# Where the values of two attention mixers get their norm scale: on GpSimd before the transposes, or on ScalarE behind them

## The chip, the cores and the metric

The kernel runs on one core of a Trainium2 chip. A core has five engines that work side by side, each with its own queue of instructions that it takes in order: TensorE (PE, matmuls and transposes; its weight loads are listed as PEld), VectorE (DVE), ScalarE (ACT), GpSimd (POOL) and SyncE (SP). An instruction that waits holds up everything behind it on its engine. Data comes from memory by DMA transfers, which are issued from SP, ACT and POOL. Matmul results land in PSUM and have to be taken out of it before its space can be used again.

The metric is the device time of one execution in microseconds (us). Lower is better. The kernel of before has a median of 891.46 us over three runs.

## The reference, cut to what matters

One step of a one-layer decoder for 512 prompt tokens and 8 sample tokens, the latter with caches. Two attention mixers read the same normalised input; their outputs are gated, summed and projected, and a channel mixer follows.

```python
def _rmsnorm(x, g):
    return x * rsqrt(mean(x * x, axis=-1) + NORM_EPS) * g     # one root per token

h = _rmsnorm(x, norm1_g)
z = h @ w_in                           # (tokens, 1024) x (1024, N_IN)
qa, ka = rope(z[q, k of mixer A])      # 16 query heads, 2 key heads of 64
va     = z[v of mixer A]               # 2 heads: 128 columns
qb, kb = rope(z[q, k of mixer B])      # 3 groups of 4 heads: 768 columns each
vb     = z[v of mixer B]               # 768 columns, no rope
# mixer A: 128 keys back, with sinks.  mixer B: group g looks back 128 keys in
# steps of 1, 4 or 16; the three outputs are weighted by their softmax sums.
# returned as well: the new cache rows, that is the k and v of the last tokens
```

The root is one number per token, and a product with a weight is linear. So the root may be left out of h and multiplied into z's rows later, in any place before the values are used.

## The kernel before, in words

**Layout.** Activations stand transposed: features on the 128 partitions, tokens along the free axis, 520 columns (512 of the prompt, 8 of the sample). `h_hi` and `h_lo` are the two parts of the input times `norm1_g`, without the root. The roots exist twice: `st[:, 10:15]`, token-major (a token per partition, one column for each of four blocks of 128 and one for the sample), and `spread`, 128 x 520, where each column holds its token's root in all 128 partitions. `cos` and `sin` have been multiplied by `spread`, so queries and keys get the root with their rotation. Values have no rotation.

**Projections.** w_in is worked through in chunks of 128 columns: qb0 to qb5, kb0 to kb5, vb0 to vb5, ka, va, qa0 to qa7, and then the gates (ga, gb) and output projections. A weight chunk is loaded (`raw_...`), split by ACT and DVE into `whi_...` and `wlo_...`, and multiplied with three matmuls for each of 8 slices of the input and each of two spans of 256 and 264 columns: 48 matmuls into a PSUM tile `ps` with the chunk's name (psvb4 is that of vb4; L292, L293, L295). The pool of these tiles, mm, has two buffers. Score tiles (sb, sa, and the small qs, ks, vs) share two buffers, transposes to token-major (tt, tsb, tps, tb) share a single one, `ps_t`.

**Values.** `evac_v` takes a value chunk out of PSUM with ACT into the work tile z and multiplies it by `spread` on POOL (L489). For the chunks of groups 1 and 2 (vb2 to vb5, `blocked`) ACT copies to a spare tile `zr` first (L492), and POOL writes z in a column order by residue of four, once for the sample's 8 columns (L493) and once for the 512 others (L494). The work tiles z and zs have two buffers each and are shared with the rotations of the keys and queries and with some gates. Then `b_tokens` and `a_tokens` transpose z four times on PE (L510, tile `tt_vb...`), ACT copies the 128 x 512 result to its place with tokens on the partitions (L561), and the 8 sample columns are transposed (L563, `vs...`) and copied by DVE. These steps are not run at once but put in the list `later`, which is worked off near the end of the next projection, so that PE has matmuls ahead of them.

**The cached scores.** Between the chunks kb0 and vb1 runs a loop over six pieces of mixer B's cache, `bs_step`: a load of queries from DRAM spread over 128 partitions (`qc`, issued by POOL, one buffer, L581), POOL's product `kc` (L586) and DVE's reduction (L587). The next qc load can start when the product is done. Behind the last piece, `bs_softmax` transposes the scores in three groups `tsb` (L607), each copied by DVE (L608) from the one `ps_t` buffer, and ACT takes the exponentials. `bs_probs` transposes the result (`tps`, L622), and DVE copies it (L623).

**Later places.** Mixer B's prompt attention follows (scores `sb` at L812 and L816), laid between the projections of va and qa. Then its tiles are closed, and mixer A starts with its scores `sa` (L946, reduced by DVE at L950), while the sample's cached keys `kca` are loaded (L1003, issued by SP), rearranged by POOL (`kpm`, L1009) and completed by a DVE copy into `kta` (L1017).

**What sets the order.** The program text gives the dependencies and a first order; a scheduler that simulates the engines fixes the order of each engine's queue when the kernel is built. So an edit at one place can change the order of instructions elsewhere, and the chip follows that order.

Of the kernel before, what the change touches and what calls it, by code (L numbers as in the profile page):

```python
# [9 lines left out]
F32 = mybir.dt.float32  # L10
F32R = mybir.dt.float32r
BF16 = mybir.dt.bfloat16
AF = mybir.ActivationFunctionType
ALU = mybir.AluOpType
AX = mybir.AxisListType

P = 128
D = 1024
NK = 8
NS = 8  # L20
NP = 512
T = NS + NP
# [44 lines left out]
def trunk_kernel(tc, x_prompt, x_sample, cache_a, cache_b1, cache_b2, cache_b3, norm1_g, w_in, sinks,  # L67
                 w_pa, w_pb, w_o, norm2_g, w_gu, w_down, final_g, cos_d, sin_d, mask_a_d, mask_b_d, mask_r_d,
                 y_p, y_s, o_pa, o_pb1, o_pb2, o_pb3, o_sa, o_sb1, o_sb2, o_sb3):
    nc = tc.nc  # L70
# [6 lines left out]
    base = root.enter_context(tc.tile_pool(name="base", bufs=1, side="left"))  # L77
# [14 lines left out]
    ident = base.tile([P, P], F32, name="ident")  # L92
# [5 lines left out]
    epst = base.tile([P, 1], F32, name="epst")  # L98
    nc.vector.memset(epst, EPS)
    g2 = base.tile([P, NK], F32, name="g2")  # L100


    copies = []
# [174 lines left out]
    later = []  # L278
# [147 lines left out]
    def norm_spread():  # L426
        for js in ((0, 1, 2, 3), (4,)):
            c0, c1 = blocks[js[0]][0], blocks[js[-1]][0] + blocks[js[-1]][1]
            bc = bank_of(f"spr{js[0]}")
            for i, j in enumerate(js):  # L430
                c, n, _ = blocks[j]
                nc.tensor.matmul(bc[:, c - c0:c - c0 + n], ones[:n, :], xstat[j][:n, :n], start=(i == 0), stop=True, skip_group_check=True)
            nc.vector.tensor_copy(spread[:, c0:c1], bc[:, :c1 - c0])
        nc.gpsimd.tensor_tensor(cos, cos, spread, op=ALU.mult)
        nc.vector.tensor_tensor(sin, sin, spread, op=ALU.mult)
# [13 lines left out]
    with tc.issue_after(steps[1, AFT[2], "a"]), tc.issue_after(steps[1, AFT[3], "v"]):  # L449
        for j in range(5):  # L450
            norm_square(j)
        norm_roots()
        norm_spread()
    nc.sync.dma_start(x_spill, x_t)
    n1ctx.close()

# [28 lines left out]
    def evac_v(ps2, name, blocked):  # L485
        z = work.tile([P, T], F32, tag="z", name="z_" + name)
        if not blocked:
            nc.scalar.activation(z, ps2, AF.Copy)
            nc.gpsimd.tensor_tensor(z, z, spread, op=ALU.mult)  # L489
        else:  # L490
            zr = work.tile([P, T], F32, tag="zs", name="zr_" + name)
            nc.scalar.activation(zr, ps2, AF.Copy)  # L492
            nc.gpsimd.tensor_tensor(z[:, NP:], zr[:, NP:], spread[:, NP:], op=ALU.mult)  # L493
            nc.gpsimd.tensor_tensor(z[:, :NP].rearrange("p (c q) -> p q c", c=4), zr[:, :NP].rearrange("p (q c) -> p q c", c=4),  # L494
                                    spread[:, :NP].rearrange("p (q c) -> p q c", c=4), op=ALU.mult)
        return z

    def unperm(ap):

# [42 lines left out]
    def b_tokens(ch, z):  # L542
        g, pr = divmod(ch, 2)
        sl = slice(pr * P, pr * P + P)

        def keys():
            ts_ = ps_s.tile([P, 512], F32, tag="s", name=f"ks{ch}")
            nc.tensor.transpose(ts_[:NS, :P], kb[:, ch, NP:], ident)
            nc.vector.tensor_copy(nat(kvb_s[:, g, 0, sl]), unperm(ts_[:NS, :P]))
            if g == 0:  # L550
                tv = to_tokens(kb[:, ch], [384], f"kb{ch}")
                nc.vector.tensor_copy(nat(k1_l[:, sl]), unperm(tv[:, 0]))
            else:
                tv = to_tokens(kb[:, ch], QORD, f"kb{ch}")
                for c in range(4):
                    nc.scalar.activation(nat(kv23[:, g - 1, c, 0, sl]), unperm(tv[:, c]), AF.Copy)

        def values():
            tv = to_tokens(z, QORD, f"vb{ch}")
            dst = v1[:, :, sl] if g == 0 else kv23[:, g - 1, :, 1, sl]  # L560
            nc.scalar.activation(dst, tv, AF.Copy)  # L561
            ts_ = ps_s.tile([P, 512], F32, tag="s", name=f"vs{ch}")
            nc.tensor.transpose(ts_[:NS, :P], z[:, NP:], ident)  # L563
            nc.vector.tensor_copy(kvb_s[:, g, 1, sl], ts_[:NS, :P])

        return keys if z is None else values

# [118 lines left out]
    def q_tokens():  # L686
# [6 lines left out]
                nc.vector.tensor_copy(nat(qb_s[:, g, pr * P:pr * P + P]), unperm(ts_[:NS, P * i:P * i + P]))  # L693
        nc.gpsimd.dma_start(q_dram, qb_s)

    later.append(q_tokens)
    loaded = {}

    def bs_step(n):
# [34 lines left out]
    def a_tokens(z):  # L734
        def go():
            tv = to_tokens(z, QORD, "va")
            nc.scalar.activation(va, tv, AF.Copy)
            tv = to_tokens(ka, [384], "ka")
            nc.vector.tensor_copy(nat(ka_l), unperm(tv[:, 0]))
            ts_ = ps_s.tile([P, 512], F32, tag="s", name="vsa")  # L740
            nc.tensor.transpose(ts_[:NS, :P], z[:, NP:], ident)
            nc.tensor.transpose(ts_[:NS, P:2 * P], ka[:, NP:], ident)
            nc.vector.tensor_copy(kva_s[:, 1], ts_[:NS, :P])
            nc.vector.tensor_copy(nat(kva_s[:, 0]), unperm(ts_[:NS, P:2 * P]))
            nc.gpsimd.dma_start(o_pa[0, 0, :, 0].rearrange("t h d -> t (h d)"), ka_l)
            nc.gpsimd.dma_start(o_pa[0, 0, :, 1].rearrange("t h d -> t (h d)"), va[:, 3])
            nc.gpsimd.dma_start(o_sa[0, :, 127].rearrange("b a h d -> b a (h d)"), kva_s)
        return go
# [863 lines left out]
```

## Time and profile before

| what | value |
|---|---|
| runs of before | 889.6, 891.46, 892.64 us; median 891.46 |
| profiled execution | 895.41 us |
| its span (first to last instruction) | 893.6 us |
| mean granted clock of TensorE | 0.985 |
| PE busy | 860.5 us (96%) |
| PE weight loads busy | 810.0 us (91%) |
| DVE busy | 536.5 us (60%) |
| ACT busy | 380.0 us (43%) |
| POOL busy | 175.9 us (20%) |

The profile is of one execution, the one of 895.41 us. A row of a group or of a timeline gives the start in us from the beginning of the span, the length in us (busy time of the group where there are several), the engine, the line of the kernel and the operation as result <- operands; `x4` means four alike in a row. In square brackets stands how long the engine was idle before, and what ended this. A row of a window begins with its start and end and the sum of the busy time; behind it come the busy times of PE, PEld, DVE, ACT and POOL, each with its number of instructions, then the granted clock as a share of full speed, the DMA engines' share and GB/s.

### The profile page before, as it was taken

How to read it: one execution, taken by the hardware profiler on the slowest of the kernel's cores; microseconds unless marked ns; L12 is line 12 of the kernel's file. 1: busy time of each engine (PE TensorE's matmuls, PEld its weight loads, DVE VectorE, ACT ScalarE, POOL GpSimd, SP SyncE). 2: the span in 40 equal slices, each digit the busy share in tenths (PEclk: the TensorE clock that was granted, in tenths of full speed). 3: DMA queues.
4: the chain of work that ended last, by engine and by line, in shares of the span. 5: the costliest groups of instructions: out<-in, count | busy, mean ns of one | idle time of the engine just before them, and what ended most of it. 6: DMA issues, size and time to landing. Idle time of an engine off the chain costs nothing.

```text
span 893.6 us, 16990 instructions
## 1 busy us (share of the span) xinstructions
PE 860.5 (96%) x6868; PEld 810.0 (91%) x6868; DVE 536.5 (60%) x1053; ACT 380.0 (43%) x782; POOL 175.9 (20%) x142
## 2 busy tenths in 40 slices
PE   6998989999999999999999799999999999999995
PEld 6898889787989888877999799999999999999995
DVE  4878638656478556552554559777534777773433
ACT  6423314434458455442332336454313455543322
POOL 2335553444325122240000021110000000000001
PEclk9999999999999999999999899999999999999998
DMA  9646755665678761599999617999985988999652
GB/s 298 183 126 183 216 167 161 196 171 143 150 177 223 206 172 30 142 240 220 288 249 283 178 48 198 322 318 284 334 306 174 329 274 273 313 320 323 217 188 96
DMA packets 166790, 194.75 MB, mean 218 GB/s; under 512 B 6936, under 2 KB 141224, under 8 KB 165304
## 3 DMA queue, kind: packets, MB, share of 16 engines
q1 hardware_dynamic: 141256, 99.40, 38.5%
q10 hardware_dynamic: 13216, 67.06, 20.6%
q0 software_dynamic: 12240, 27.22, 15.5%
q8 instruction: 54, 0.88, 0.4%
q14 instruction: 24, 0.20, 0.1%
HBM read 186.81 MB, written 93.81 MB: 314 GB/s over the span
## 4 chain that ended last, share of the span: by engine, by line
PE 79%; DMA 8%; DVE 6%; POOL 2%; issue 2%; ACT 1%; POOLq 0%; SPq 0%; ACTq 0%; DVEq 0%
PE pse L1511 3%; PE poa L978 3%; PE pse L1512 3%; PE pse L1514 3%; PE psb L1365 2%; PE psa L1367 2%; PE pse L1365 2%; PE psb L1367 2%; PE pse L1367 2%; PE psb L1366 2%; PE psa L1365 2%; PE pse L1366 2%; PE psa L1366 2%; DMA raw_wo<-in_w_o 2%; DMA qc<-q_dram 2%; PE psqa L292 2%
## 5 line engine op out<-in xcount | busy, mean ns | idle before, releaser
L1332 ACT ACTIVATE whi<-rawp 128x1024 fp32r<-128x1024 f32 x94 | 97.7, 1041 | 144.2 <-PE psb L1366 35.4
L1333 DVE TENSOR_TENSOR wlo<-rawp,whi 128x1024 fp32r<-128x1024 f32 x94 | 112.8, 1201 | 44.0 <-ACT whi L1332 40.1
L1511 PE MATMUL pse<-g,whi 128*128 128x260 f32 x192 | 52.6, 291 | 0.7 <-DVE x L1499 0.7
L1512 PE MATMUL pse<-g,whi 128*128 128x260 f32 x192 | 50.7, 282 | 0.0
L960 POOL TENSOR_TENSOR pa<-pa,sta 128x1024 f32<-128x1024 f32 (+1 forms) x16 | 29.6, 1848 | 93.6 <-DVE sta L959 60.7
L1366 PE MATMUL psb<-ht_lo,whi 128*128 128x260 f32 x160 | 45.2, 283 | 0.0
L1367 PE MATMUL psb<-ht_hi,wlo 128*128 128x260 f32 x160 | 45.2, 283 | 0.0
L1365 PE MATMUL psb<-ht_hi,whi 128*128 128x260 f32 x160 | 45.2, 283 | 0.0
L1365 PE MATMUL psa<-hb_hi,whi 128*128 128x260 f32 x160 | 45.1, 282 | 0.0
L1367 PE MATMUL psa<-hb_hi,wlo 128*128 128x260 f32 x160 | 45.1, 283 | 0.0
L1366 PE MATMUL psa<-hb_lo,whi 128*128 128x260 f32 x160 | 45.0, 281 | 0.0
L292 PE MATMUL pso<-m_hi,whi_wo 128*128 128x260 f32 x128 | 36.3, 294 | 4.6 <-DVE x L1142 4.6
L1514 PE MATMUL pse<-g,wlo 128*128 128x260 f32 x192 | 40.7, 283 | 0.0
L1511 PEld LDWEIGHTS pse<-g,whi 128*128 128x128 f32 x192 | 36.2, 188 | 1.0 <-DVE x L1499 0.9
L292 PE MATMUL psqa<-h_hi,whi_qa 128*128 128x256 f32 (+1 forms) x128 | 36.6, 304 | 0.0
L1425 POOL DMA_DIRECT2D yts<-in_final_norm_g x1 | 0.6, 590 | 181.5 <-PE psb L1367 181.5
L1512 PEld LDWEIGHTS pse<-g,whi 128*128 128x128 f32 x192 | 36.2, 188 | 0.0
L293 PE MATMUL pso<-m_lo,whi_wo 128*128 128x260 f32 x128 | 36.2, 292 | 0.0
L293 PE MATMUL psqa<-h_lo,whi_qa 128*128 128x256 f32 (+1 forms) x128 | 35.8, 298 | 0.0
L292 PE MATMUL psga<-h_hi,whi_ga 128*128 128x256 f32 (+1 forms) x128 | 34.9, 293 | 0.3 <-ACT whi_ga L182 0.3
L293 PE MATMUL psga<-h_lo,whi_ga 128*128 128x256 f32 (+1 forms) x128 | 34.7, 289 | 0.0
L293 PE MATMUL psgb<-h_lo,whi_gb 128*128 128x256 f32 (+1 forms) x128 | 34.5, 287 | 0.0
(446 smaller groups left out, 3102.8 us busy)
## 6 DMA issues: line engine op xcount, KB each, us to landing
rawp<-in_w_gu SPq DMA_DIRECT2D x30, 512.0 KB, 7.0
rawp<-in_w_down SPq DMA_DIRECT2D x16, 512.0 KB, 6.7
out<-in_cache_b_kv ACTq DMA_DIRECT2D x8, 1022.0 KB, 7.7
out<-in_cache_b_kv ACTq DMA_DIRECT2D x8, 512.0 KB, 5.1
raw_qa<-in_w_in SPq DMA_DIRECT2D x8, 512.0 KB, 7.8
raw_ga<-in_w_in SPq DMA_DIRECT2D x8, 512.0 KB, 8.0
raw_gb<-in_w_in SPq DMA_DIRECT2D x8, 512.0 KB, 6.2
raw_pa<-in_w_pa SPq DMA_DIRECT2D x16, 256.0 KB, 11.6
```

Source lines behind the costliest of these rows:

```text
L292: nc.tensor.matmul(ps[i], hi[:, k], xh[:, k0 + k, sl], start=st, stop=False)
L293: nc.tensor.matmul(ps[i], hi[:, k], xl[:, k0 + k, sl], start=False, stop=False)
L960: last_pool[0] = nc.gpsimd.tensor_tensor(p[:, :, m0:], p[:, :, m0:], st[:, 5].unsqueeze(2).to_broadcast([P, 4, 256 - m0]), op=ALU.mult).ins
L978: nc.tensor.matmul(po[64 * kv:64 * kv + 64, :], va[:, j - 1 + r, 64 * kv:64 * kv + 64], pts_[kv, r], start=(r == rel[0]), stop=(r == 1), s ...
L1332: a = nc.scalar.activation(hi, raw, AF.Copy)
L1333: nc.vector.tensor_tensor(lo, raw, hi.bitcast(F32), op=ALU.subtract)
L1365: nc.tensor.matmul(pss[e], h, xh[:, j, i], start=start and i == 0, stop=False, skip_group_check=True)
L1366: nc.tensor.matmul(pss[e], h, xl[:, j, i], start=False, stop=False, skip_group_check=True)
L1367: nc.tensor.matmul(pss[e], l, xh[:, j, i], start=False, stop=i == 3, skip_group_check=True)
L1511: nc.tensor.matmul(ps[h], hi[:, k], gh[:, sl], start=st, stop=False)
L1512: nc.tensor.matmul(ps[h], hi[:, k], gl[:, sl], start=False, stop=False)
L1514: nc.tensor.matmul(ps[h], lo[:, k], gh[:, slice(*SPAN2[h])], start=False, stop=en)
```

## The change

The values are transposed as they come out of the matmuls. The root is applied behind the transpose, when ACT copies them: there a token stands on each partition, and an ACT copy takes a scale per partition.

- A tile `roots` (128 x 9) is added: columns 0 to 3 hold the roots of the prompt's tokens in plain order, column 8 those of the sample, both copied by DVE from `st`. Columns 4 to 7 hold the roots in the order by residue. They come from `strided_roots`: four PE transposes of `spread` and one DVE copy, put in `later` behind `q_tokens`.
- `evac_v` loses POOL's products: 11 instructions. For the blocked chunks, ACT writes z itself, in two pieces and with the strided order, without `zr`.
- The copy behind the transposes (`scaled`) is four ACT instructions of 128 x 128, each with a column of `roots` as its scale, instead of one of 128 x 512; seven times.
- The copies of the sample's values become DVE multiplications by `roots[:NS, 8:9]`.

```diff
+    roots = base.tile([P, 9], F32, name="roots")
...
         norm_spread()
+        nc.vector.tensor_copy(roots[:, 0:4], st[:, 10:14])
+        nc.vector.tensor_copy(roots[:NS, 8:9], st[:NS, 14:15])
...
         z = work.tile([P, T], F32, tag="z", name="z_" + name)
         if not blocked:
             nc.scalar.activation(z, ps2, AF.Copy)
-            nc.gpsimd.tensor_tensor(z, z, spread, op=ALU.mult)
         else:
-            zr = work.tile([P, T], F32, tag="zs", name="zr_" + name)
-            nc.scalar.activation(zr, ps2, AF.Copy)
-            nc.gpsimd.tensor_tensor(z[:, NP:], zr[:, NP:], spread[:, NP:], op=ALU.mult)
-            nc.gpsimd.tensor_tensor(z[:, :NP].rearrange("p (c q) -> p q c", c=4), zr[:, :NP].rearrange("p (q c) -> p q c", c=4),
-                                    spread[:, :NP].rearrange("p (q c) -> p q c", c=4), op=ALU.mult)
+            nc.scalar.activation(z[:, NP:], ps2[:, NP:], AF.Copy)
+            nc.scalar.activation(z[:, :NP].rearrange("p (c q) -> p q c", c=4), ps2[:, :NP].rearrange("p (q c) -> p q c", c=4), AF.Copy)
         return z
+
+    def scaled(dst, tv, first):
+        for c in range(4):
+            nc.scalar.activation(dst[:, c], tv[:, c], AF.Copy, scale=roots[:, first + c:first + c + 1])
...
             tv = to_tokens(z, QORD, f"vb{ch}")
             dst = v1[:, :, sl] if g == 0 else kv23[:, g - 1, :, 1, sl]
-            nc.scalar.activation(dst, tv, AF.Copy)
+            scaled(dst, tv, 4 if g else 0)
             ts_ = ps_s.tile([P, 512], F32, tag="s", name=f"vs{ch}")
             nc.tensor.transpose(ts_[:NS, :P], z[:, NP:], ident)
-            nc.vector.tensor_copy(kvb_s[:, g, 1, sl], ts_[:NS, :P])
+            nc.vector.tensor_scalar_mul(kvb_s[:, g, 1, sl], ts_[:NS, :P], roots[:NS, 8:9])
...
+    def strided_roots():
+        tp = ps_t.tile([P, 512], F32, tag="t", name="trt")
+        for c in range(4):
+            nc.tensor.transpose(tp[:, P * c:P * c + P], spread[:, c:NP:4], ident)
+        nc.vector.tensor_copy(roots[:, 4:8], tp.rearrange("p (c f) -> p c f", f=P)[:, :, 0])
+
     later.append(q_tokens)
+    later.append(strided_roots)
...
             tv = to_tokens(z, QORD, "va")
-            nc.scalar.activation(va, tv, AF.Copy)
+            scaled(va, tv, 0)
...
-            nc.vector.tensor_copy(kva_s[:, 1], ts_[:NS, :P])
+            nc.vector.tensor_scalar_mul(kva_s[:, 1], ts_[:NS, :P], roots[:NS, 8:9])
```

Behind the new tile the lines move by one to eleven: L489 becomes L491, L510 becomes L514, L608 becomes L612, L622 becomes L626, L812 becomes L823, L950 becomes L961 and L1017 becomes L1028.

The edit also moves other instructions. Three places show it; a number behind a name is only that of the buffer, and the brackets name the engines or DMA queues that a row waits for.

**POOL, in the loop of the cached scores while the chunks vb0 and vb1 run.** Before:

```order
L581 DMA qc20_1118<-q_dram_314 128x4x256 [waits Pool_49]
L489 TENSOR_TENSOR z_vb0_1270<-z_vb0_1270,spread_111 128x520 [waits Activation_49]
L586 TENSOR_TENSOR kc20_1116<-kc20_1116,qc20_1118 128x1024 [waits DMAHW6_49,DMASW6_49]
L581 DMA qc24_1199<-q_dram_314 128x4x256 [waits Pool_49]
L489 TENSOR_TENSOR z_vb1_1340<-z_vb1_1340,spread_111 128x520 [waits Activation_49]
L586 TENSOR_TENSOR kc24_1197<-kc24_1197,qc24_1199 128x1024 [waits DMAHW0_49,DMASW7_49]
L796 DMA out_7<-kvb_s_311 8x512 [waits DVE_49]
```

After:

```order
L585 DMA qc20_1127<-q_dram_317 128x4x256 [waits Pool_49]
L590 TENSOR_TENSOR kc20_1125<-kc20_1125,qc20_1127 128x1024 [waits DMAHW6_49,DMASW6_49]
L585 DMA qc24_1208<-q_dram_317 128x4x256 [waits Pool_49]
L590 TENSOR_TENSOR kc24_1206<-kc24_1206,qc24_1208 128x1024 [waits DMAHW0_49,DMASW7_49]
L807 DMA out_7<-kvb_s_314 8x512 [waits DVE_49]
```

The two products with `spread` no longer stand between the load of a piece and the work on the pieces.

**PE, where chunk ka ends and va begins.** Before, the transposes of vb3 and vb4 and those of vb5's sample columns stand spread within va's 48 matmuls; this is the piece around the first of them:

```order
L295 MATMUL psva_1780<-h_hi_104,wlo_va_1687 128x264
L292 MATMUL psva_1780<-h_hi_104,whi_va_1686 128x256
L293 MATMUL psva_1780<-h_lo_105,whi_va_1686 128x256
L292 MATMUL psva_1780<-h_hi_104,whi_va_1686 128x264
L293 MATMUL psva_1780<-h_lo_105,whi_va_1686 128x264
L510 MATMUL tt_vb3_1585<-ident_84,z_vb3_1525 128x128 [waits DVE_49]
L510 MATMUL tt_vb3_1585<-ident_84,z_vb3_1525 128x128 x3
L295 MATMUL psva_1780<-h_hi_104,wlo_va_1687 128x256
L295 MATMUL psva_1780<-h_hi_104,wlo_va_1687 128x264
```

After, they stand together ahead of va's first matmul, with the twelve small transposes `tps` and a first group of mixer B's scores:

```order
L626 MATMUL tps_1525<-ident_84,sr_319 128x8 x8
L296 MATMUL pska_1704<-h_hi_105,wlo_ka_1623 128x256
L296 MATMUL pska_1704<-h_hi_105,wlo_ka_1623 128x264
L514 MATMUL tt_vb3_1597<-ident_84,z_vb3_1539 128x128 [waits DVE_49]
L514 MATMUL tt_vb3_1597<-ident_84,z_vb3_1539 128x128 x3
L514 MATMUL tt_vb4_1677<-ident_84,z_vb4_1615 128x128 [waits Activation_49]
L514 MATMUL tt_vb4_1677<-ident_84,z_vb4_1615 128x128 x3
L567 MATMUL vs5_1750<-ident_84,z_vb5_1697 8x128 [waits Activation_49]
L823 MATMUL sb000_1869<-kb_310,qb_309 32x256 x4
L827 MATMUL sb000_1869<-kb_310,qb_309 128x128 x2
L293 MATMUL psva_1797<-h_hi_105,whi_va_1700 128x256 [waits Activation_49]
```

Two matmuls of ka are left between `tps` and the transposes of vb3, and none between those of vb3 and of vb4.

**DVE, where mixer A's first scores are reduced.** Before:

```order
L474 STREAM_SHUFFLE zs_qa7_2805<-z_qa7_2804 128x520 [waits Activation_49]
L950 ISA pa000_2859,sta000_2860<-sa0000_2861,mask_a_112 128x128 [waits PE_49]
...
L950 ISA pa000_2859,sta000_2860<-sa0001_2874,mask_a_112 128x128
L950 ISA sta000_2860 128x1
L1017 COPY kta_3128<-ka_293 128x8 [waits DMAHW6_49,Pool_49]
L938 TENSOR_TENSOR qs011_3044<-qa_292,qs011_3044 64x512 [waits Activation_49]
```

After:

```order
L477 STREAM_SHUFFLE zs_qa7_2824<-z_qa7_2823 128x520 [waits Activation_49]
L1028 COPY kta_3147<-ka_296 128x8 [waits DMAHW6_49,Pool_49]
L961 ISA pa000_2878,sta000_2879<-sa0000_2880,mask_a_113 128x128 [waits PE_49]
...
L961 ISA pa000_2878,sta000_2879<-sa0001_2893,mask_a_113 128x128
L961 ISA sta000_2879 128x1
L949 TENSOR_TENSOR qs011_3063<-qa_295,qs011_3063 64x512 [waits Activation_49]
```

The copy into `kta`, which waits for the load of `kca` and for POOL, has moved ahead of the four reductions.

## The prediction

> **What bounds the kernel now.** I read the page's totals first, then the list of what PE waited for, then the chain that ended last in 80 to 270 us.
>
> ```profile
> span 893.6 us, 16990 instructions
> PE 860.5 (96%) x6868; PEld 810.0 (91%) x6868; DVE 536.5 (60%) x1053; ACT 380.0 (43%) x782; POOL 175.9 (20%) x142
> ...
> PE pso L292 <- DVE x L1142: 4.6, 1, 4.6
> PE tt_vb L510 <- POOL z_vb L489: 3.3, 2, 2.5
> ```
>
> PE is busy for 860.5 of 893.6 us. An edit here pays only where PE stands still, or where its clock is low. POOL, which loses work, is busy 20% of the time: the scaling taken off it is worth nothing by itself. What counts is the 3.3 us for which PE waited for that scaling.
>
> ```profile
> 103.92 3.31 POOL kc L586
> 107.51 6.28 DMA qc<-q_dram
> 113.87 2.41 POOL kc L586
> 117.37 1.30 POOL z_vb L489
> 118.72 0.66 PE tt_vb L510 x4
> 124.83 0.44 PE tsb L607 x4
> 128.48 0.44 PE tsb L607 x4
> 129.64 0.24 PE psvb L295 x2
> 130.37 0.24 PE psvb L295 x2
> 144.62 0.84 PE tps L622 x12
> 153.82 0.57 PE sb L812 x8
> 154.39 0.64 PE sb L816 x4
> 181.22 1.68 PE pos L660 x16
> 248.10 11.32 DMA kca<-in_cache_a_kv
> 259.59 1.25 POOL kpm L1009 x2
> ```
>
> This is the chain in order of time (start, length). Up to 118.7 it isn't PE's: it is the loop of the cached scores, a qc load of some 6 us, POOL's product kc, the next load. The scaling of chunk vb1 is queued behind it, and PE behind the scaling. From 118.7 to 248 the chain is PE alone, six projection matmuls in 0.73 us (129.64 to 130.37), 0.12 each. At 248.10 it leaves PE for the load of kca.
>
> **The stall that goes.**
>
> ```profile
> 109.68 0.66 PE L510 MATMUL tt_vb<-ident,z_vb 128*128 128x128 f32 x4 [0.79 <-POOL z_vb L489]
> 118.72 0.66 PE L510 MATMUL tt_vb<-ident,z_vb 128*128 128x128 f32 x4 [2.53 <-POOL z_vb L489]
> 109.66 0.58 ACT L488 ACTIVATE z_vb<-psvb 128x520 f32<-128x520 f32 x1
> 120.00:124.00 4.00, 4.00 (x23) 4.00 (x22) 1.23 (x2) 0.01 (x1) 2.69 (x2) 0.57 0.86 277
> ```
>
> ACT had vb1's copy ready at 110.24, so without POOL's product neither group of transposes waits: 0.79 + 2.53 = 3.32 us. The last row is a window: PE busy all 4.00 us, yet at a granted clock of 0.57. It stands right behind the 2.53 us gap, so I let it go with the gap: 4.00 x 0.43 = 1.72 us. Together PE gains 5.04 us by the middle of chunk vb4.
>
> [...]
>
> **What is late next.** PE now runs into the same qc loop at another place. The three groups of tsb share one PSUM tile, so the second waits for DVE's copy of the first (L608), and that copy stands in DVE's queue behind the last cached reduction (L587).
>
> ```profile
> 121.31 2.36 POOL L586 TENSOR_TENSOR kc<-kc,qc 128x1024 f32<-128x1024 f32 x1 [2.65 <-DMA qc<-q_dram]
> 123.70 1.22 DVE L587 TENSOR_REDUCE st_b<-kc 128x16 f32<-128x1024 f32 x1 [2.77 <-POOL kc L586]
> 125.31 0.68 DVE L608 COPY sr<-tsb 8x512 f32<-8x512 f32 x1 [0.39 <-PE tsb L607]
> ```
>
> POOL's last product started when its load landed, not when POOL was free, so it stays where it is, L587 ends at 124.92 and the copy at 125.60. PE comes to its first transposes at 118.72 - 3.32 = 115.40, adds 0.52 for them and 37 rows of 0.12 (tsb stands 5 rows later now), 0.44 for tsb, 27 rows: 124.04. It waits 1.56 us. So of 5.04 us, 3.48 are left. A lower price (0) needs an earlier load; a higher one has no row.
>
> The four new transposes of the spread tile and DVE's copy of them cost PE about 0.44 us (as tsb's four), some 60 us earlier, and POOL no step. They only use up part of that 1.56 us wait: nothing. If they delayed the loop itself, they would cost up to 0.44 + 0.68.
>
> **The values' chain, vb3 to vb5.** Two things change on ACT.
>
> ```profile
> 104.73 0.79 ACT L556 ACTIVATE kv<-tt_kb 128x128 f32<-128x128 f32 x4 [1.34 <-PE tt_kb L510]
> 148.78 0.60 ACT L561 ACTIVATE kv<-tt_vb 128x512 f32<-128x512 f32 x1 [0.60 <-PE tt_vb L510]
> 191.83 0.18 ACT L664 ACTIVATE ob_hi<-pos 128x16 fp32r<-128x16 f32 x1
> L492 ACT ACTIVATE zr_vb<-psvb 128x520 f32<-128x520 f32 x4 | 2.3, 584 | 0.0
> L861 ACT ACTIVATE ob_hi<-pob 128x512 fp32r<-128x512 f32 x2 | 2.2, 1113 | 5.7 <-PE pob L855 5.7
> 145.50 0.26 DVE L623 COPY pts<-tps 128x96 f32<-128x96 f32 x1 [1.42 <-PE tps L622]
> ```
>
> The token copy is four activations of 128x128 instead of one of 128x512: 0.79 for 0.60, seven times, +1.3 us of ACT. The blocked evacuation (four chunks) is two activations: 0.18 for the 8 samples, and 128x512 with a strided result, between 0.584 (L492, plain) and 1.113 (L861, strided, the nearer): +0.2 to +0.7 each. In all +2 to +4 us on an engine that is busy 43%. The cover is that ACT waits for PE around here; where it is gone is one place.
>
> Before, ACT emptied psvb5 into a spare tile at once. Now it writes z itself, which has two buffers, so the evacuation of vb5 waits until PE has transposed vb3; it stands in ACT's queue ahead of the copy for vb4 and of z_ka, and va's projection takes over vb5's PSUM tile. The new order therefore puts tps, tt_vb3, tt_vb4, vs5 and a score group ahead of psva, with hardly a projection row between. On PE: tps ends; DVE's copy takes 0.04 + 0.26, and about 0.1 to be seen, two rows (0.24) lie beside it: 0.2 idle. After tt_vb3 (0.44), tt_vb4 waits for four scaled copies, 0.79 + 0.2 of passing on, about 1.1 idle. The evacuation, 0.18 + 1.11, runs beside tt_vb4 (0.44) and the score group (0.57 + 0.64): nothing more is lost if vs5, between them, needs only the 8 samples' part, up to 0.75 if it needs all. Lower end 0.9 (the short waits hidden), upper 2.1; I take 1.5, as the strided row is the nearer one.
>
> **The kca barrier.** DVE's kta copy (L1017) waits for kca's load and POOL's kpm; it moves ahead of the first four score reductions (L950).
>
> ```profile
> 257.03 0.28 DVE L950 CUSTOM_DVE_ANT_0 pa<-sa,mask_a 128x128 f32<-128x128 f32 x1
> 260.86 1.26 DVE L1017 COPY kta<-ka 128x8 f32<-128x8 f32 x1 [2.30 <-POOL kpm L1009]
> 258.81 0.23 PE L946 MATMUL sa<-k_hi,qs 128*128 128x128 f32 x1
> 265.94 0.39 PE L946 MATMUL sa<-k_hi,qs 128*128 128x256 f32 x1 [1.75 <-DVE sta L950]
> 266.00:270.00 4.00, 4.00 (x22) 4.00 (x23) 3.80 (x19) 3.84 (x14) 1.29 (x2) 0.61 0.69 165
> ```
>
> Counted from 248.10, where kca starts, DVE did L950 from +8.9 to +10.5, waited, and had kta done at +14.0. In the new order it idles from +8.9, has kta at +14.0 and only then the reductions. The score tiles have two buffers, so PE's third group (now at +10.7, as 258.81) waits for the first reduction: to +14.5, 3.7 us. The group that waited 1.75 us at +17.8 then comes at +18.4 (14.0, the reductions with zs between 1.5, 2.4 of other rows, 0.4) with 11 projection rows (1.3) fewer done. Loss 0.6 + 1.3 = 1.9 us. If kca lands early, the loss is a gain of the old 1.75 and of the slow stretch behind it (4.00 x 0.39 = 1.6); if the longer gap costs a second slow stretch, the loss is 1.9 + 1.6 = 3.5. I take 1.9.
>
> **Sum.** -5.04 + 1.56 + 0 + 1.5 + 1.9 = -0.1 us. The profiled execution took 895.41 us for its span of 893.6; it would take 895.3. The median of the three runs, 891.46, lies 3.95 us under that execution; I carry the difference over: **891.4 us**, no change. About 0.3%, 2.7 us, is what a measurement of this kernel can tell.
>
> **Rivals.** *Faster, the barrier opens early.*
>
> ```profile
> raw_qa<-in_w_in SPq DMA_DIRECT2D x8, 512.0 KB, 7.8
> raw_ga<-in_w_in SPq DMA_DIRECT2D x3, 512.0 KB, 9.7
> ```
>
> kca is 512 KB and took 11.32 us; others of that size took 7.8 (page) and 9.7 (three issues just ahead of kca). At 9.7 the barrier's loss is 0.3, 889.8. It decides below about 8.7 us; at 7.8 DVE finds kpm ready and the result is 891.46 - 3.48 + 1.5 - 3.35 = 886.1. I price it at 887.5. For it: the new order puts fewer rows between psqa6 and this point, so other transfers move. Against: those transfers move with kca.
>
> *Slower, the clock.* One mechanism: short or narrow matmuls lower the granted clock even where PE never waits.
>
> ```profile
> 184.00:189.00 5.00, 5.00 (x30) 4.97 (x30) 3.80 (x7) 1.72 (x3) 1.62 (x2) 0.66 1.07 223
> ```
>
> This window follows the 16 tiny matmuls of 181.22. The new cluster tps to sb, 4.8 us with two gaps, is of the same kind, and the kca gap is longer: two stretches of 1.7 us more, 894.8. It decides when both fall. Against: later score groups lie further apart in the new order, and the old stretch at 185 may go.
>
> *The change doesn't do what it says:* tt_vb still waits, now for ACT, where z_vb stands behind a weight split of about 1 us. Then the 5.04 is lost, but also the 1.56: 895 us. Against it, ACT's row at 109.66 is 5 us early.
>
> *Given back later:* PE stands 4.6 us before pso at 506, behind weight loads. If these keep their hour, an earlier PE gains nothing there, but none is forecast.
>
> **How the numbers follow.** Forecast (-2.7 to +2.7) 0.42. Early barrier 0.25, and 0.04 for both terms of loss hidden without it (888.0): faster 0.29. Clock 0.23, doesn't do it 0.06: slower 0.29. The likeliest case's own range is 888.8 to 894.1. To leave out no more than 2 in 10, the range reaches into the early barrier to 887.2 and into the clock to 895.2.
>
> **What would show it.** Right: no wait of tt_vb on POOL; a wait of the second tsb on L608's copy of 1 to 2 us, with PE 3 to 4 us earlier there; idle PE of 1 to 2 us between tps and psva; DVE waiting over 3 us at kta, and PE at the third score group. Wrong: kca landing in under 9 us, psva directly behind pska without a gap, or more than one slow stretch more or fewer up to 280 us.

## The result, and the profile after

The changed kernel takes 898.54 us in the median of four runs (892.49 to 904.32), the kernel before 890.53 us beside it. The ratio is 1.0101, with a 95% interval of 1.0056 to 1.0146: **slower**, where no change (891.4) was forecast and 895.2 was the upper end of the range. A repeat (below) has a median of 899.12 us over twelve runs, against 890.34 for the kernel before, a ratio of the medians of 1.0099; five of its executions lie over 900 us and are left out of the ratio and interval that are given there, since the comparison drops what is over 1.5% above the fastest.

The profiled execution is one of the shorter ones: 894.56 us, span 892.8, clock 0.985, against 895.41, 893.6 and 0.985 of the one before. So the two totals say nothing here, and the profile has to be read by place. First the waits of PE in the changed kernel (who waited for what: us in all, times, longest):

```profile
PE ta L981 <- ACT pta L983: 9.2, 1, 9.2
PE xtp L403 <- DMA xt<-in_x_prompt: 6.2, 2, 3.5
...
PE pso L293 <- ACT whi_wo L183: 1.6, 1, 1.6
...
PE tt_vb L514 <- ACT z_vb L493: 1.2, 1, 1.2
```

The wait of tt_vb on POOL is gone, and so is that of sa on DVE (1.75 before). A wait of 9.2 us stands on top, at a place of which the forecast said nothing: mixer A's last transposes, near 391 us. (`ta` is the PSUM tile of these transposes and `pta` ACT's copy of it; `poa` is mixer A's output, `pa` and `ga` name weights and tiles of the projections around it, and `pso` is the tile of the last projection of this part, near 460 to 530 us.) The timelines of POOL, SP, ACT and PE there show its parts:

```profile
376.98 1.89 POOL L971 TENSOR_TENSOR pa<-pa,sta 128x1024 f32<-128x1024 f32 x1 [7.59 <-DVE sta L970]
378.81 3.76 POOL L142 DMA_DIRECT2D sum_s1B<-in_w_gu  x3
379.89 0.37 SPq L165 DMA_DIRECT2D raw_ga<-in_w_in  x1
398.70 1.06 ACT L183 ACTIVATE whi_ga<-raw_ga 128x1024 fp32r<-128x1024 f32 x1 [11.41 <-DMA raw_ga<-in_w_in]
399.66 0.58 ACT L983 ACTIVATE pta<-ta 128x512 f32<-128x512 f32 x1
400.39 1.09 PE L981 MATMUL ta<-ident,pa 128*128 128x128 f32 x4 [9.19 <-ACT pta L983]
```

POOL finishes mixer A's last product and issues three transfers that add weight columns into `sum_s1B` in memory, 768 KB each. One us later SP issues the load of the second late gate's weights, `raw_ga`, 512 KB. It lands after 18.7 us. ACT's split of it (L183) stands in ACT's queue ahead of the copy of the transposed probabilities (`pta`), and PE stands behind that copy. The same four places before:

```profile
384.13 0.37 SPq L164 DMA_DIRECT2D raw_ga<-in_w_in  x1
388.01 2.87 POOL L960 TENSOR_TENSOR pa<-pa,sta 128x1024 f32<-128x1024 f32 x1 [4.19 <-ACT whi_ga L182]
388.45 1.06 ACT L182 ACTIVATE whi_ga<-raw_ga 128x1024 fp32r<-128x1024 f32 x1 [0.58 <-DMA raw_ga<-in_w_in]
390.82 3.74 POOL L141 DMA_DIRECT2D sum_s1B<-in_w_gu  x3
```

There the load was issued at 384.13 and had landed (4.2 us) before the adds began at 390.82. The change brought the load 4.2 us forward and the adds 12.0 us. Most of these 12 us are order: before, two weight splits of ACT (whi_pb6 and whi_pb7) stood between mixer A's last two groups of exponentials; now four splits stand behind the last group. ACT's row right behind the last exponentials, before and in the changed kernel:

```profile
386.25 0.57 ACT L972 ACTIVATE pta<-ta 128x512 f32<-128x512 f32 x1
```

```profile
374.27 0.58 ACT L983 ACTIVATE pta<-ta 128x512 f32<-128x512 f32 x1
```

POOL's product follows the exponentials, and the adds, which wait for nothing else, follow the product.

The theory taken into the runs, **collision**: the change itself is worth about nothing, as the sum had it, and the loss comes from these adds, which now run into a weight load. Rivals: **luck** (one slow load in one execution), and **bytes** (the stage from 380 to 512 us is bound by its loads, so that PE's lead is given back there in any case).

### The profile page after: what moved, and what is told of

Its sections match the earlier page's. It is cut to its first block, busy times and chain, and to the rows that moved or that the text cites. A ratio compares the mean times of both kernels' runs of the same rounds, so it can differ in the third digit from the quotient of the medians.

```text
span 892.8 us, 17018 instructions
## 1 busy us (share of the span) xinstructions
PE 857.5 (96%) x6872; PEld 807.2 (90%) x6872; DVE 532.7 (60%) x1056; ACT 385.3 (43%) x807; POOL 164.9 (18%) x131
## 4 chain that ended last, share of the span: by engine, by line
PE 83%; DMA 5%; DVE 5%; issue 2%; POOL 1%; ACT 1%; POOLq 0%; SPq 0%; ACTq 0%; DVEq 0%
PE pse L1522 3%; PE pse L1523 3%; PE poa L989 3%; PE pse L1525 3%; PE psb L1376 2%; PE psa L1378 2%; PE psb L1377 2%; PE psb L1378 2%; PE pse L1377 2%; PE psa L1377 2%; PE psa L1376 2%; PE pse L1378 2%; PE pse L1376 2%; DMA raw_ga<-in_w_in 2%; PE psgb L296 2%
## 5 line engine op out<-in xcount | busy, mean ns | idle before, releaser
L1523 PE MATMUL pse<-g,whi 128*128 128x260 f32 x192 | 50.9, 282 | 0.0
L968 ACT ACTIVATE pa<-pa,sta 128x256 f32<-128x256 f32 (+1 forms) x64 | 30.0, 471 | 15.3 <-DVE sta L964 15.2
L293 PE MATMUL psgb<-h_hi,whi_gb 128*128 128x256 f32 (+1 forms) x128 | 34.4, 288 | 0.0
```

What stands on the lines that cost most here:

```text
L293: nc.tensor.matmul(ps[i], hi[:, k], xh[:, k0 + k, sl], start=st, stop=False)
L968: nc.scalar.activation(p[:, i, m0:], p[:, i, m0:], AF.Exp, bias=st[:, 1, i:i + 1], scale=SC, accum_out=st[:, 4, i:i + 1])
L1523: nc.tensor.matmul(ps[h], hi[:, k], gl[:, sl], start=False, stop=False)
```

## The experiments

A result lists for each execution its span and its mean granted clock. Span times clock is taken as an estimate of what the span would have been at full clock, and the rest of the span as one of what the slow clock cost; below, "full" and "slow" are these two, as means over a run's executions (a span of 887.0 at 0.987 is 875.5 and 11.5).

### The collision: the same again, held, and put into the kernel before

**e1, the changed kernel once more**, no edit.

> The changed kernel once more, for a second profile and more times. Collision theory: the change brings PE some 7 us ahead by 386 us and mixer A's last POOL product 11 us ahead (377 instead of 388 us); the three 768 KB adds into sum_s1B that stand behind it in POOL's queue now start one us ahead of the load of raw_ga, which takes 18.7 us instead of 4.2, and PE waits 9.2 us plus about 2 at the halved clock. It is in the order of the program, so it must show again: an idle PE of 5 to 11 us around 391 us behind a load of raw_ga of over 12 us; times 892 to 904, median 1.0 to 1.5% over the kernel before. Luck theory (one slow load in one execution): no such wait, raw_ga lands in under 9 us, times within 0.3% of before.

Measured: 899.12 us over twelve runs (886.71 to 905.57), ratio 1.0041 (1.0001 to 1.0081). The profiled execution was the shortest of the twelve, and has the wait too:

```profile
PE ta L981 <- ACT pta L983: 8.9, 1, 8.9
```

Not luck. Over all twelve, full is 881.9 and slow 14.1, against 879.0 and 10.0 of the 29 runs of the kernel before beside it: 2.9 us are lost at full clock and 4.1 by the clock. Over the seven executions up to 900 us it is 881.3 and 11.1, a loss of 2.3 and 1.1. So this run puts the loss somewhere between 3 and 9 us, and not all of the 9 us wait reaches the end: at pso, where PE waited 4.6 us before, it waits 2.2 in the first profile of the changed kernel and not at all in this one.

**e2 and e10, the adds held.**

```diff
+HOLD = 49
...
-          {"s1": (37, 38, 39, 48), ...
+          {"s1": (37, 49, 49, 49), ...
...
             name, kc, _, sp = jobs[i]
             load_to(i + 2)
+            if i == HOLD:
+                last_pool[0] = nc.gpsimd.tensor_copy(roots[:, 9:10], raws[i][0][:, 0, 0:1]).ins
```

POOL's queue gets one tiny copy ahead of the three adds; a few rows of ACT, PE and DVE between 384 and 416 us swap, and nothing else moves.

> The changed kernel, but POOL first copies one column of the second raw_ga tile before it issues the three adds into sum_s1B, so these start when that load has landed. Collision theory: raw_ga lands in 4 to 9 us, PE waits under 3 us around 391, keeps its lead of about 7 us against the kernel before at the first pa matmul, and the time falls by 5 to 11 us against the changed kernel: 884 to 892 us, faster than before or equal to it. Rival (the stage from 380 to 512 us is bound by the bytes of its loads, so that a lead is given back there wherever the adds stand): the wait appears at raw_wo or raw_wg between 470 and 510 us, and the time stays within 3 us of the changed kernel's.

> The changed kernel with held adds once more, beside the plain half with held adds and on the same chip, for the size of the change without the collision: 887 to 891, within 0.3% of the kernel before.

Measured: 889.14 us (882.63 to 894.88), ratio 0.9989 (0.9954 to 1.0024), and again 890.7 us, ratio 0.999 (0.9957 to 1.0023). In the first of the two, the timeline of POOL, and then what PE waited for from 376 to 440 us:

```profile
382.33 0.19 POOL L267 COPY roots<-raw_ga 128x1 f32<-128x1 f32 x1 [5.21 <-DMA raw_ga<-in_w_in]
382.57 3.77 POOL L143 DMA_DIRECT2D sum_s1B<-in_w_gu  x3
```

```profile
PE psga L296 <- ACT whi_ga L184: 1.5, 1, 1.5
PE psga L299 <- DVE wlo_ga L185: 0.4, 1, 0.4
```

One tiny instruction takes 10.0 us off the changed kernel's median (899.12 to 889.14): full falls from 881.9 to 877.6, slow from 14.1 to 9.8. Against the seven executions up to 900 us alone (median 894.49) it is 5.4 us. The bytes theory, by which the time would have stayed within 3 us of the changed kernel's, fails. A part of it holds, though: in this profile PE waits 1.1 us at pso, in the second 4.8, as in the kernel before (4.6), so a lead is given back there in some executions. With this wait gone the change makes no difference that can be measured.

The hold does not make the adds harmless, though: it chooses which loads they meet. In the same profile the raw_ga issued at 384.86, behind the held adds, lands after 21.9 us and a raw_pa after 24.2. ACT waits 6.65 us for the first, but PE has other matmuls in the meantime, and the 1.5 us at psga above is all that it waits for this load:

```profile
406.85 1.06 ACT L184 ACTIVATE whi_ga<-raw_ga 128x1024 fp32r<-128x1024 f32 x1 [6.65 <-DMA raw_ga<-in_w_in]
```

In the kernel before, too, a raw_pa issued behind the adds took 14.4 us, and PE did not wait for it.

**e3, the collision put into the kernel before.** In its text the adds are placed behind mixer A's last product; one line lets them go ahead of it.

```diff
-        last_pool[0] = nc.gpsimd.tensor_tensor(p[:, :, m0:], ...).ins
+        mul = nc.gpsimd.tensor_tensor(p[:, :, m0:], ...).ins
+        if (qd, j, kv) != (1, 3, 1):
+            last_pool[0] = mul
```

POOL's product moves behind the three adds; every other row of every engine is the same.

> The kernel before, with one edit: the three adds into sum_s1B stand ahead of mixer A's last product in POOL's queue instead of behind it (some 384 instead of 391 us). Nothing else moves on any engine. Collision theory: the load of raw_ga that is issued at about 384 us now takes 10 to 18 us instead of 4.2, PE waits 5 to 11 us for it near 391, and the time grows by 3 to 10 us, less what the later wait at pso (4.6 us and 1.7 of halved clock) takes up: 892 to 900 us. Rival (bound by the bytes): PE waits near 391 but correspondingly less at 506, and the time is within 0.3% of before.

Measured: 900.71 us (894.5 to 903.94), ratio 1.0103 (1.0056 to 1.0151). The load that suffers is not the one named. That raw_ga was issued 0.4 us behind the first add and still took 4.2 us; of the loads issued later, the next raw_ga took 22.4 and raw_pa 23.6. The timeline of ACT, and then PE's wait for the copy behind it:

```profile
400.19 1.06 ACT L182 ACTIVATE whi_pa<-raw_pa 128x1024 fp32r<-128x1024 f32 x1 [12.42 <-DMA raw_pa<-in_w_pa]
...
401.15 0.58 ACT L974 ACTIVATE pta<-ta 128x512 f32<-128x512 f32 x1
```

```profile
PE poa L980 <- ACT pta L974: 6.2, 1, 6.2
```

So the adds alone, without any part of the change, cost the kernel before as much as the change did (890.34 to 900.71 in the median). What suffered here are loads issued later behind them (22.4 and 23.6 us), and PE paid 6.2 us where it needed one of these soon.

**e6, the control**: the kernel before with the same held adds.

> The control: the kernel before with the same held adds as the first of these runs (a POOL copy from the second raw_ga tile ahead of the three adds). In before the adds start 2.5 us after that load has landed anyway, so the hold changes little: 888 to 893, within 0.3% of the kernel before. What the change is worth when the adds can't run into the load is then the difference between the changed kernel with held adds (889.1) and this one: about -1 us by the forecast's sum (-0.1), -4 to -5 by the lead that the profiles show at 376 us (17.8 us of waits and slow clock against 22.2).

Measured: 888.88 us, as the kernel before beside it (888.88); ratio 1.0021 (0.9992 to 1.005). The changed kernel with held adds is at 0.9989 and 0.999 by the same measure. The difference, 0.3% or 2.8 us in favour of the change, is no larger than the intervals on either side: when the adds can't strike, it is not shown that the change is worth anything, and the 4 to 5 us that the leads in the profiles suggested are neither shown nor excluded.

**e5, the adds one by one**, behind the second, third and fourth late raw_ga tile: `"s1": (37, 49, 51, 53)`, with a POOL copy at each.

> As the run with the held adds, but the three adds into sum_s1B are held one by one: each waits for a POOL copy of one column of another raw_ga tile (the second, third and fourth of the late gates), so that no three of them run together. Collision theory: no load of raw_ga or raw_pa between 375 and 410 us takes over 14 us (24.2 with the adds together behind the second raw_ga), PE waits under 2 us in 376 to 440, and the median is 885 to 889, at or below the run with the adds held together (889.1) and 10 to 14 us below the changed kernel (899.1). Rival (only the load right behind the second raw_ga matters): within 1.5 us of the adds held together. Rival (bytes): a new wait at pso between 460 and 510 of over 4 us, median 892 or more.

Measured: 892.42 us (883.6 to 898.75), ratio 1.0025 (0.9986 to 1.0064), and the profile is of the longest of its twelve executions (898.75). No load issued from 375 to 410 us took over 11.0, as the collision theory had it, but a raw_pa issued at 410.3 took 23.2. PE waits 3.1 us at pspa and 6.2 at pso. The theory's time is missed, and what came is what the bytes rival named, a wait of over 4 us at pso and a median over 892: to spread the adds over the stage brings nothing over holding them. That it loses 3 us is not shown, since the intervals overlap.

### Half of the change at a time

**e4, the plain half.** `evac_v`, the token copies and the sample's copies are changed for vb0, vb1 and va only; vb2 to vb5 are as before.

> Half of the change: the root is moved behind the transposes only for the chunks in plain order (vb0, vb1, va); vb2 to vb5 are scaled by POOL from the spare tile as before. The wait of the transposes of vb0 and vb1 on POOL (3.3 us, and 1.7 of halved clock) must go, and the group tps to psva must not stand in one piece. If the change is decided by where the adds fall against raw_ga: PE ahead by 3 to 6 us at 380, and the end depends on whether a raw_ga load is issued within 5 us of the adds: if so 894 to 902, if not 883 to 889. If the strided evacuation is what costs the time: 884 to 889 in either case.

Measured: 894.08 us, ratio 1.0043 (1.0015 to 1.0072). Here too a load behind the adds is late (raw_pa, 18.8 us), and PE waits 4.0 us for `pta`.

**e8 and e12, the plain half with held adds**, the same edit as in e2.

> The plain half of the change (vb0, vb1 and va scaled behind the transposes, vb2 to vb5 by POOL as before) with the three adds held until the second raw_ga tile has landed. In the plain half alone the load of raw_pa that was issued just behind the adds took 18.8 us, and PE waited 4.0 us and lost 1.7 by the clock. Collision theory: that load lands in under 12 us, PE waits under 2 us in 376 to 420, and the median falls from 894.1 by 4 to 8 us to 886 to 890, equal to the kernel before or faster. Rival (the plain half itself costs time): the wait near 400 goes, but the median stays over 892.

> The plain half with held adds once more, to see whether its lead over the kernel before (0.9911) holds on another set of runs: 884 to 888, 0.4 to 1.0% under the kernel before, beside the run with the small transposes later.

Measured: 886.39 us, ratio 0.9911 (0.9874 to 0.9948), and again 882.44 us, ratio 0.9911 (0.9878 to 0.9944); in the second, one of the seven executions, the profiled one, took 4673.5 us and is left out of the ratio. This version is **0.9% faster than the kernel before**, in both sets of runs. What PE waited for from 376 to 440 us in the first of the two is 0.9 us in all:

```profile
PE pspa L296 <- DVE ta L1126: 0.9, 1, 0.9
```

**e7 and e9, the strided half**: vb2 to vb5 changed, the rest as before.

> The other half of the change: only vb2 to vb5 get the root behind the transposes (ACT writes z strided, four scaled copies); vb0, vb1 and va are scaled by POOL as before. The transposes of vb0 and vb1 wait for POOL again (1.4 to 3.3 us). Collision theory: what this half costs or gains at the end is decided by where its order puts the three adds against the loads of raw_ga and raw_pa: a load of over 15 us and a wait of PE of 4 to 10 us in 376 to 410 go with 895 to 902, their absence with 888 to 893. If instead the strided evacuation and the four copies cost the time, the median is over 895 without such a wait, and PE's lost time between 114 and 256 us is over 6 us.

> The strided half of the change (vb2 to vb5) once more, for a second profile. Its first one had no collision, but 10.3 us of halved clock between 140 and 200 us, in stretches of 3.6 and 7.2 us, the first behind an idle gap of 1.7 us of PE between the small transposes and va. If it is this half's order that brings the slow clock, the second profile shows at least 5 us of it there again and the time is 894 to 900; if it was one execution's chance, under 3.5 us and the time is 888 to 893.

Measured: 898.72 us, ratio 1.0107 (1.0069 to 1.0145), and 896.5 us over eight runs, ratio 1.0031 (0.9985 to 1.0077). PE waits 1.1 and 0.9 us from 376 to 440, so no late load holds it there. The time goes earlier. Windows of the first (length; busy time of PE, PEld, DVE, ACT and POOL; granted clock; share and GB/s of DMA):

```profile
144.00:148.00 4.00, 2.31 (x22) 1.54 (x21) 3.89 (x5) 3.44 (x10) 0.56 (x1) 1.00 0.73 211
148.00:156.00 8.00, 8.00 (x43) 7.68 (x40) 6.12 (x12) 2.41 (x9) 2.50 (x2) 0.57 0.68 260
156.00:200.00 44.00, 44.00 (x328) 36.63 (x327) 27.70 (x58) 15.95 (x39) 18.69 (x16) 0.84 0.65 179
```

PE stands 1.7 us, then runs 8 us at a clock of 0.57 and 44 us at 0.84: 3.4 and 7.0 us lost without a wait. The second profile has some 6.8 there, over the 5 that its expectation asked for. Four means of runs made side by side:

| kernel | full | slow |
|---|---|---|
| before (24 runs) | 879.7 | 9.6 |
| plain half, adds held (e8, 7) | 875.8 | 6.9 |
| whole change, adds held (e10, 12) | 879.1 | 9.9 |
| strided half (e9, 8) | 880.5 | 13.0 |

With the adds held, the plain half is worth 6.6 us, 3.9 at full clock and 2.7 by the clock, and with the strided half added to it nothing of this is left.

**e11, is it the gap at 143 us?** In the whole change with held adds the small transposes are put on the list one chunk later, so that tps to va no longer stands in one piece.

```diff
-        if ch == 2:
+        if ch == 3:
             later.append(bs_probs)
```

> The whole change with held adds, and one more line: the small transposes tps are put on the list one chunk later, so that the group from tps to va's first matmul no longer stands in one piece (the transposes of vb4 and vb5 lie within va, as they did before the change). Other rows move too. Theory that the strided half costs its time by the idle gap at 143 us and the slow clock that follows in 145 to 200 (1.2 + 3.4 us in both profiles with held adds, 8.5 to 12 in the two of the strided half): idle and slow clock of 140 to 200 us fall under 2.5 us, and the median is 885 to 888, like the plain half with held adds. Rival (the price lies in the strided writes and the four copies, or elsewhere): 888 to 893 as with the held adds alone.

Measured: 894.79 us, ratio 1.0065 (1.0031 to 1.0098). Two windows of it:

```profile
140.00:156.00 16.00, 16.00 (x143) 13.94 (x141) 14.89 (x26) 7.14 (x18) 3.75 (x4) 1.00 0.91 264
174.80:188.80 14.00, 14.00 (x70) 13.46 (x63) 5.09 (x11) 2.92 (x8) 4.85 (x4) 0.51 0.90 228
```

The gap is gone, and the clock is full there; but a stretch of 14 us at half clock follows, with PE busy all the time. PE also waits 5.4 us from 376 to 440, here not for a late load (the two raw_ga before it took 3.9 and 3.8 us) but in the main for DVE's split (2.5) and ACT's copy pta (1.8). The profile is of the longest of the twelve executions (902.93), so its 14 us are not the usual case; but the median missed the theory's 885 to 888 as well. That the gap is the strided half's price is not borne out, with the limit that other rows moved too.

**e13, without ACT's direct write.** As e2, but vb2 to vb5 go through `zr` again, and POOL copies them to z in the strided order, unscaled; the four scaled copies stay.

> The whole change with held adds, but vb2 to vb5 are emptied as before: ACT copies the PSUM tile to the spare tile zr, and POOL copies zr to z in the strided order (unscaled); the four scaled copies behind the transposes stay. It separates the two edits of the strided half. If ACT's direct strided write into z is what costs the whole change with held adds (889 to 891) its 6 us against the plain half with held adds (882 to 886), by the group it forces ahead of va: the gap of 1.2 us at 143 us is gone and the time is 882 to 887. If the four scaled copies or the rest of the order cost it: 888 to 893, with the slow clock between 156 and 200 us as in the other runs of the strided half (1.7 to 6.9 us).

Measured: 888.72 us, ratio 0.9998 (0.9966 to 1.003). The gap is gone, the slow clock from 156 to 200 us costs 1.7, and yet the time is that of the whole change with held adds; in its profile PE waits 6.2 us at pso. So neither the direct write nor the gap is shown to be what the strided half costs. That stays open: what the runs show is only that it costs some 6 us against the plain half, partly by the clock. One rival was not tested. The pso stage, which neither half edits, took 50.9 us in the plain half's profile (e8) and 49.2 in the first of the whole change with held adds (e2), but 54.4 in the second (e10) and 55.9 here (first to last matmul); e13 reaches it only 1.5 us behind e8. Whether the strided half's order brings this about or single executions differ, these profiles can't tell.

## Why the prediction was wrong, step by step

- **What failed: "Given back later: ... none is forecast"**, and with it the sum that stops at the kca barrier, at some 270 us. The new order was followed on PE and DVE up to there, but not on ACT, POOL and SP behind it, where ACT's splits, POOL's adds and SP's loads stand in new places to each other. What stood there instead is a wait of 9.2 us. The runs put the missing term at +5 to +10 us: 10.0 by the medians with one copy on POOL (e2), 5.4 without the executions over 900 us, and 10.4 in the kernel before when its adds go ahead (e3, 890.34 to 900.71). The rival of this name looked at pso only; the place was 115 us ahead of it.
- **The sum of -0.1** lies within what the change measures with the adds held (0.9989 and 0.999, intervals of 0.3% to either side). That is luck: its terms were off in both directions, as the next points show.
- **The stall that goes (-5.04)**: right in mechanism; no profile of the changed order waits for POOL at tt_vb. The size came from one execution. Two other profiles of the old order (e3, e6: the same rows up to 376 us) have 1.4 and 1.2 us there, and no slow clock behind it; the second one of the strided half (e9), where vb1 is scaled as before, has the same gap of 2.5 us and still a full clock behind it. So the term is anything from 1.2 to 5.0. PE's list of waits in e3:

```profile
PE tt_vb L510 <- POOL z_vb L489: 1.4, 1, 1.4
```

- **The new wait at tsb (+1.56)**: the place and the size are right in two of five profiles of the changed order (1.4 us in e5 and e10), and there is none in the other three. "It stays where it is" failed: without the scaling between them POOL's steps came earlier, the last product at 119.25 instead of 121.31 (POOL's timeline of the changed kernel, and then a row of PE's waits in e10).

```profile
119.25 2.37 POOL L590 TENSOR_TENSOR kc<-kc,qc 128x1024 f32<-128x1024 f32 x1 [4.10 <-DMA qc<-q_dram]
```

```profile
PE tsb L614 <- DVE sr L615: 1.4, 1, 1.4
```

- **The chain vb3 to vb5 (+1.5)**: right. tt_vb4 waits 1.2 us (1.1 forecast, though the 0.79 and 0.2 that it was added up from make 1.0) in all five profiles; the 0.2 us behind tps does not show. In four of the five a stretch of halved clock follows, 1.7 us that the term does not hold. PE's timeline in the changed kernel:

```profile
143.48 0.66 PE L514 MATMUL tt_vb<-ident,z_vb 128*128 128x128 f32 x4 [1.23 <-ACT z_vb L493]
```

- **The kca barrier (+1.9)**: wrong in sign. kca landed in 5.8 us instead of 11.3 (issued at 242.6), DVE's copy found its input ready, and both the old wait of 1.75 us and the slow stretch behind it are gone, as the rival "the barrier opens early" had it (a gain of 3.35). "Those transfers move with kca" is the sentence that failed: POOL's add into sum_s3A, which had been issued 2.0 us ahead of kca, comes 0.5 us behind it. The rows of POOL and SP, two of the kernel before and two of the changed one:

```profile
246.11 1.55 POOL L141 DMA_DIRECT2D sum_s3A<-in_w_gu  x1
248.10 0.37 SPq L1003 DMA_DIRECT2D kca<-in_cache_a_kv  x1
```

```profile
242.55 0.37 SPq L1014 DMA_DIRECT2D kca<-in_cache_a_kv  x1
243.01 1.54 POOL L142 DMA_DIRECT2D sum_s3A<-in_w_gu  x1
```

From kca's issue to POOL's use of it, the three profiles with the add 2.0 us ahead have 11.2 to 11.5 us, two with it 3.4 ahead 10.0 to 10.3 (e11, e13), two with it 6.7 ahead 8.5 to 8.6 (e4, e8), and the five with it just behind 4.9 to 5.8. So the gain here and the loss near 390 us look like one thing, a load that meets an add; no run moves this add alone. The timelines of POOL and DVE in the changed kernel:

```profile
248.38 2.15 POOL L1020 COPY kpm<-kca 128x512 f32<-128x512 f32 x2 [3.83 <-DMA kca<-in_cache_a_kv]
252.18 0.14 DVE L1028 COPY kta<-ka 128x8 f32<-128x8 f32 x1
```

- **The clock as a rival**: half right. Slow stretches did come behind the new cluster (0.50 from 145.8 to 149.2 us) and behind tiny matmuls (0.57 from 179.6 to 183.6), but the kernel before has as many of the kind (0.53 from 157.6 to 161.2 and from 184.8 to 188.4). The changed kernel's extra slow time over all its executions (14.1 against 10.0) goes with the collision, since it is gone with it (9.8). In the strided half alone the rival is what happens (13.0 against 9.6).
- **The chances**: slower was given 0.29, by other mechanisms than the one that came.

## What to carry to other kernels

An edit that lets a scheduler write a new order has to be followed to the end of the program, on every queue that issues transfers: find each large transfer that nothing holds back but its place in a queue, and ask what load stands next to it now. A bulk transfer off the critical path can be pinned to where it does less harm by one tiny instruction that reads what must land first: here a copy of 0.19 us on POOL took 10.0 us off the median, or 5.4 without the executions over 900 us (e2). And a stall that one profile shows is a sample (here the wait at tt_vb: 2.5 us in the profile of before, 1.4 in e3 and 1.2 in e6): before its size goes into a sum, take a second profile of the same order.

## What the hardware showed that was not expected

**A load beside the adds.** The same 512 KB load took 4.2 us ahead of the three adds of 768 KB and 18.7 right behind them; other loads in that place took 18.8 (e4) and 23.6 us (e3), and with the adds held 21.9 and 24.2 (e2). What that cost differed with how soon PE needed the load: 9.2 us of waiting in the changed kernel, 1.5 in e2. An issue on SP was long as well: this row of the changed kernel is one issue of 8.73 us, where the other loads of raw_ga near it take 0.37 to 0.42.

```profile
386.61 8.73 SPq L165 DMA_DIRECT2D raw_ga<-in_w_in  x1
```

Why the loads beside the adds were slow, no run here shows.

**The slow clock comes in portions.** In the two profiles of before and after, taken in windows of 0.4 us, TensorE's granted clock falls to 0.50 for 3.4 us or for a multiple: before, four times for 3.4 us (from 120, 158, 185 and 267 us) and once for 6.8 (from 506); in the changed kernel three times for 3.4 us (from 146, 180 and 357) and once for 10.2 (from 395). Each 3.4 us lost 1.7. The longest stretch is the one of 14 us at 0.51 in e11. The clock fell behind a gap of 1.2 us of PE in the changed kernel, but not behind a like one in its repeat (e1; PE is busy for 2.77 of the 4 us from 142 to 146 in both). The windows behind these gaps, the first in the changed kernel, the second in e1:

```profile
145.80:149.20 3.40, 3.40 (x18) 3.40 (x17) 3.40 (x9) 0.05 (x1) 1.59 (x2) 0.50 0.70 281
```

```profile
146.00:150.00 4.00, 4.00 (x35) 3.95 (x34) 4.00 (x9) 1.34 (x6) 1.70 (x2) 1.00 0.74 297
```

And it fell with no gap at all: PE was busy throughout the 6.8 us ahead of the stretch at 185 us before, and throughout the 7.6 ahead of the one at 180 in the changed kernel. Both, and the window of 14 us in e11, come behind 16 very small matmuls of 128x1 (from 181.1, 176.4 and 172.6 us). Such stretches go with a spread of 10 us and more between executions of one kernel (e1: from 886.71 us at a clock of 0.994 to 905.57 at 0.980), and twelve of them still leave a ratio open by 0.3 to 0.4% to either side (e2, e1).
